# A hybrid decoder layer whose mixer input is scaled by its norm and split a second time, slice by slice

## The chip, the core and the metric

The kernel runs on one core of a Trainium2 chip. The metric is the device time of one execution in microseconds (us), the median of several runs. A core has TensorE (PE, matrix products into PSUM), VectorE (DVE), ScalarE (ACT), GpSimd (POOL) and SyncE (SP, which here only issues transfers). Each engine works through its own list of instructions in a fixed order; semaphores make one wait for another.

## The reference

One decoder layer on 512 tokens of 1024 channels, in float32: `h = x + SwiGLU(norm(x))/2`, then `h = h + mixer(norm(h))`, then `h = h + SwiGLU(norm(h))/2`, then a last norm. The norm before the mixer and the projection behind it are what the change is about:

```
y = xf * lax.rsqrt(jnp.mean(xf * xf, axis=-1, keepdims=True) + EPS); return y * g
proj = (u @ w_in)
(hq, hf, hi, hg, gq, gk, gv, ga, gb, gz, gate_h, gate_g) = jnp.split(proj, offsets)
```

The columns of the projection feed an HGRN2 branch (8 heads; q, forget gate f, values i, output gate g), a gated delta-rule branch (8 key heads, 16 value heads; q, k, v through a short causal convolution, two scalars per head and token, an output gate z) and two merge gates. Each branch is a recurrence over chunks of tokens, gets a norm of its own, is projected back, and the two are merged and projected once more. The root of the norm is one number per token, so it may be applied to the projection's input or to each of its outputs.

## The kernel before

Activations lie channel by token: `h` is eight slices of 128 channels by 512 tokens. A product in float32 is made of three products in a reduced form of float32: both operands are split into a high part (a cast on ScalarE) and a low part (a subtraction on VectorE), and `mm3` (L165 to L168) multiplies high by high, high by low and low by high into one PSUM bank. The split input of the mixer is `uh`, `ul`. Weights come in slabs of 128 by 512 (`raw`, 256 KB), and each slab is cast and subtracted likewise (`whi`, `wlo`, in `maker`, L1865 and L1867).

Before the change `uh` and `ul` hold `h` times the norm's gain, without its root. The root is found while the first columns are being multiplied: sums of squares by token (`pst`, L1971), a power on GpSimd (`rcol`, one number per token in token-major form), a product that spreads it (`pbc`) and a copy (`rbc`, 128 by 512, L1987). Every output of the projection is then multiplied by it when it leaves its bank: by `rbc` on VectorE where the tile is channel by token (`h_q`, `h_f`, `conv`, `tgate`, `decays`), by `rcol` as a factor of ScalarE's activation where it is token by channel (`h_v`, `gate`), and in the two output norms (`h_head`, `g_rec`), where the value columns' factor is still missing.

The order of work is written by a planner, `Desk`, which runs when the program is built: each piece of work is a thread that asks for an engine for a modelled time or for a buffer, and Desk records instructions in the order in which its modelled engines take them. That order is then fixed. The dense columns come in the order of the list `DENSE`, of which `choose` takes the first whose conditions hold: F and Q (forget gate and q of an HGRN head), B (values and gate of two heads), D (the scalars), k, q, v and z of the delta branch, y (the HGRN branch's way back), and where none can be taken, one of 16 merge gate tiles t0 to t15. What it took before the change: F0 Q0 F1 Q1 B0 F2 Q2 F3 Q3 B1 D0 F4 F5 Q4 Q5 B2 F6 F7 t0 Q6 Q7 B3, then k0 to v1, z0, y0 to y7, then the rest of k, q, v and z with t1 to t3 among them, t4 to t15 behind z7, and last the projection of the delta branch (`closing`). Small products of heads and recurrences stand between the large ones.

PSUM has eight banks: two for dense tiles (`mm`), two each in lanes a and b, one each in d and e. A channel-by-token tile is 24 matmuls of 512 columns in one bank; the next tile goes to the other `mm` bank while the first is emptied. B is four such tiles, one per block of 128 tokens, each over all eight slices of the input, so its eight slabs are all needed within its first tile; half of them lie in buffers of their own (`EXTRA`). The first feed-forward block opens differently (`opening`): four tiles in four banks, slice by slice, three matmuls in each bank for each slice.

Of the kernel before, what the change touches and what calls it, by code (L numbers as in the profile page):

```python
# [37 lines left out]
)  # L38
MERGE = (None, None, "a", "a", "b", "b", None, None)
LATE = 1  # L40
WB = 6
EXTRA = ((1, 3, 5, 7), (1, 3, 5, 7), (1, 3, 5, 7), (5, 7))
TA = 6
RB = 3
KEEP = 2
# [76 lines left out]
        assert not self.asked, [(th.rank, th.want) for th in self.asked]  # L122


def body(tc, xT, cst, sqc, hmask, dta, w1o, w1a, w2a, wt, wn, wab, wbh, wbg, wo, w1b, w2b, yT, dbg=None):
    nc = tc.nc
    pe, act, dve, pool, sp = nc.tensor, nc.scalar, nc.vector, nc.gpsimd, nc.sync
    ctx = ExitStack()
# [22 lines left out]
    rcol, rhalf = rcols[:, 0:4], rcols[:, 8:12]  # L151


    def slab(src):
# [662 lines left out]
def mixer(tc, mp, e):  # L817
    nc = tc.nc
    pe, act, dve, pool, sp = nc.tensor, nc.scalar, nc.vector, nc.gpsimd, nc.sync
    cs, ident, tri, strict, hm, ones, mhalf = (e[k] for k in ("cs", "ident", "tri", "strict", "hm", "ones", "mhalf"))  # L820
    uh, ul, rbc, rcols, rcol, rhalf, h = (e[k] for k in ("uh", "ul", "rbc", "rcols", "rcol", "rhalf", "h"))
    psc, dr, dense, slab, wp, mm3, ux, hd, dbg = (
        e[k] for k in ("psc", "dr", "dense", "slab", "wp", "mm3", "ux", "hd", "dbg"))
    wt, wn, wab, wbh, wbg, wo, dta, psd = (e[k] for k in ("wt", "wn", "wab", "wbh", "wbg", "wo", "dtab", "psd"))

    def ps(name, lane="d"):
        return psc.tile([P, T], F32, tag="p" + lane, name=name, bufs=LANES[lane])
# [77 lines left out]
    def decays(pab):  # L905
# [3 lines left out]
        pool.memset(ab, 0.0)  # L909
        z = h[:64, 1]  # L910
        z2 = h[:16, 2]
        yield "on", "rbc"
# [6 lines left out]
        dve.tensor_tensor(z, z, rbc[:64], op=ALU.mult)  # L919
# [62 lines left out]
        D.fire("decays")  # L982


    def h_q(i, pt):
        yield "get", "ta", 2
        yield "on", "rbc"
        yield *V(512), 1
        qs = ta("qs")
        dve.tensor_tensor(qs, pt, rbc, op=ALU.mult)  # L990
# [9 lines left out]
        D.put("ta", 2)  # L1000
        D.fire(("Q", i))

    def h_f(i, pt):
        yield "get", "ta", 1
        yield "on", "rbc"
        yield *V(512), 1
        fs = ta("fs")
        dve.tensor_tensor(fs, pt, rbc, op=ALU.mult)
        D.put("mm")
        yield A(512)  # L1010
        act.activation(fs, fs, AF.Tanh, scale=0.5)
# [12 lines left out]

    def h_v(i, t, o):
        yield A(300)
        act.activation(hv_[i][:, t], o, AF.Copy, scale=rcol[:, t:t + 1])
        if t == 3:
            D.fire(("V", i))

    def h_head(i):
# [148 lines left out]
        yield V(4)  # L1180
        dve.tensor_tensor(rho, rho, rcol, op=ALU.mult)
# [30 lines left out]
    def conv(k, i, pt, out, n):  # L1212

        yield "get", "ta", 2
        yield *V(512), 1
# [3 lines left out]
        D.put("mm")  # L1219
# [234 lines left out]
    def g_rec(u, st):  # L1454
# [95 lines left out]
        yield "use", "POOL", 2.2  # L1550
        pool.tensor_tensor(rho, rho, mhalf[:, :8], op=ALU.pow)
        pool.tensor_tensor(v3(rho, 2), v3(rho, 2), mid(rcol, 2), op=ALU.mult)
        yield "lag", EASE
        ons = []
        for i in range(2):
# [40 lines left out]
    def tgate(i, pt):  # L1596

        yield "get", "ta", 1
        yield *V(512), 1
        g = ta("tg")  # L1600
        dve.tensor_tensor(g, pt, rbc, op=ALU.mult)
        D.put("mm")
        yield A(512)
# [12 lines left out]
        D.put("mm")  # L1616
        D.start((6, d), keep(md[d], g, "ta", ("y", d)))

    def gate(key, g, t, o):

        yield "get", "thg", 1
        yield A(300)
        th = places["thg"]("thg", (P, 256))
        act.activation(th, o, AF.Tanh, scale=rhalf[:, t:t + 1])
        yield V(256)
        dve.scalar_tensor_tensor(g[:, t], th, 1.0, o, op0=ALU.add, op1=ALU.mult)
        D.put("thg")
        if key[0] == "G" or t % 2:
            D.put("mm")
        if t == 3:  # L1630
            D.fire(key)

# [205 lines left out]
    def maker(key, raw):  # L1838
# [31 lines left out]
        yield "lag", .4  # L1870
        D.fire(("slab", key))

    def product():
        for n in range(len(todo) + len(gates) + len(line)):
            yield "on", ("line", n + 1)
            x = k, i = line[n]
            if k == "B":
# [3 lines left out]
                hg_[i] = place("gz", "hg", (P, NT, 256), 4)  # L1881
                for t in range(NT):
                    yield "get", "mm", 1
                    for kt in range(KD):
# [77 lines left out]
    def norm():  # L1962
# [16 lines left out]
        yield V(4)  # L1979
        dve.tensor_scalar(rhalf, rcol, 0.5, None, op0=ALU.mult)  # L1980
        yield "get", "d", 1
        yield T_(.9)
        pb = ps("pbc")
# [72 lines left out]
def layout(i):  # L2056
# [27 lines left out]
    def ffn(n):  # L2084
# [9 lines left out]
        w1a=w1a, w2a=w2a, wt=wt, wn=wn, wab=_kpn(wab).reshape(P, -1),  # L2094
# [18 lines left out]
```

## Time and profile before

| what | value |
|---|---|
| median of 3 runs | 1624.95 us (1624.8 to 1631.92) |
| the profiled execution | 1623.19 us |
| its span, first to last instruction | 1621.4 us |
| TensorE busy | 1599.5 us (99%), 11170 matmul instructions |
| VectorE, ScalarE, GpSimd busy | 1134.0, 858.5, 414.6 us |
| TensorE's granted clock, mean | 0.997 |

An engine's busy time is the sum of its instructions; idle time is put down to what released the engine. PE and PEld are TensorE's matmuls and weight loads. The start of a matmul lies before the end of the one ahead of it, so the distance of starts tells the pace, not the length of one.

### The profile page before, as it was taken

What the parts mean: (1) busy time and instruction counts of PE and PEld (TensorE: products, weight loads), DVE (VectorE), ACT (ScalarE), POOL (GpSimd) and SP (SyncE); (2) the same over time, 40 slices, a digit from 0 to 9 for tenths busy, and PEclk for the clock granted to TensorE, in tenths of its full rate; (3) what the DMA queues carried; (4) which work ended last, traced back from release to release, by engine and by line L of the source; (5) the groups of instructions that cost most, each with busy time, mean ns of one, the idle gap of its engine ahead of it and who ended that gap; (6) DMA issues with size and microseconds to landing.
All of it is one profiled execution on the core that took longest, in us unless ns stands there. A gap on an engine that the chain in (4) does not pass through costs nothing.

```text
span 1621.4 us, 30263 instructions
## 1 busy us (share of the span) xinstructions
PE 1599.5 (99%) x11170; PEld 1408.9 (87%) x11170; DVE 1134.0 (70%) x2166; ACT 858.5 (53%) x1853; POOL 414.6 (26%) x744
## 2 busy tenths in 40 slices
PE   8999999999999999999999999999999999999997
PEld 7999998887878788888888988888888899999887
DVE  7877774547677778658888888755545877778353
ACT  7766663332434435456566565553325766667232
POOL 0222210101121221254571666510001322220012
PEclk9999999999999999999999999999999999999999
DMA  5988843532312222443323333445545888883343
GB/s 177 236 185 183 183 104 98 172 114 86 104 40 73 88 76 90 129 147 98 102 90 110 104 102 121 150 137 185 159 143 163 192 201 183 184 185 79 115 136 117
DMA packets 128165, 216.52 MB, mean 134 GB/s; under 512 B 21888, under 2 KB 27776, under 8 KB 128016
## 3 DMA queue, kind: packets, MB, share of 16 engines
q1 hardware_dynamic: 110448, 182.89, 35.6%
q0 software_dynamic: 17280, 31.46, 12.8%
q8 instruction: 88, 1.44, 0.4%
q14 instruction: 61, 0.50, 0.1%
q10 hardware_dynamic: 288, 0.22, 0.1%
HBM read 197.45 MB, written 17.07 MB: 132 GB/s over the span
## 4 chain that ended last, share of the span: by engine, by line
PE 92%; DMA 3%; issue 1%; ACT 1%; DVE 1%; POOL 0%; SPq 0%; DVEq 0%; ACTq 0%; POOLq 0%
PE pmm L166 16%; PE pmm L167 15%; PE pmm L168 15%; PE pnat L166 4%; PE pnat L168 4%; PE pnat L167 4%; PE pfa L166 3%; PE pfa L167 3%; PE pfa L168 3%; PE pfx L166 2%; PE pfx L168 2%; PE pfx L167 2%; PE pfy L168 2%; PE pfy L167 2%; PE pfy L166 2%
## 5 line engine op out<-in xcount | busy, mean ns | idle before, releaser
L166 PE MATMUL pmm<-uh,whi 128*128 128x512 f32 x632 | 264.4, 418 | 5.6 <-ACT whi L709 5.6
L1865 ACT CAST whi<-raw 128x512 fp32r<-128x512 f32 x226 | 140.1, 620 | 214.5 <-PE pmm L167 156.8
L1867 DVE TENSOR_TENSOR wlo<-raw,whi 128x512 fp32r<-128x512 f32 x226 | 160.6, 711 | 128.3 <-ACT whi L1865 121.8
L168 PE MATMUL pmm<-uh,wlo 128*128 128x512 f32 x632 | 248.2, 393 | 0.0
L167 PE MATMUL pmm<-ul,whi 128*128 128x512 f32 x632 | 247.9, 392 | 0.0
L420 DVE TENSOR_TENSOR sig<-h,sig 128x1024 fp32r<-128x1024 f32 x80 | 97.7, 1221 | 70.4 <-ACT sig L418 70.4
L166 PEld LDWEIGHTS pmm<-uh,whi 128*128 128x128 f32 x632 | 119.5, 189 | 27.1 <-ACT whi L709 5.6
L168 PEld LDWEIGHTS pmm<-uh,wlo 128*128 128x128 f32 x632 | 119.2, 189 | 26.3
L166 PE MATMUL pmm<-gh,whi 128*128 128x512 f32 (+1 forms) x374 | 140.9, 377 | 0.0
L168 PE MATMUL pmm<-gh,wlo 128*128 128x512 f32 (+1 forms) x374 | 140.9, 377 | 0.0
L167 PE MATMUL pmm<-gl,whi 128*128 128x512 f32 (+1 forms) x374 | 140.8, 377 | 0.0
L167 PEld LDWEIGHTS pmm<-ul,whi 128*128 128x128 f32 x632 | 119.7, 189 | 20.4 <-DVE ul L193 0.2
L418 ACT CAST sig<-h 128x1024 fp32r<-128x1024 f32 x80 | 83.9, 1049 | 88.1 <-PE pfa L168 85.1
L204 POOL TENSOR_TENSOR acc<-acc,sqt 128x512 f32<-128x512 f32 x18 | 24.1, 1338 | 376.4 <-ACT sqt L202 376.3
L166 PE MATMUL pnat<-whi,uh 128*128 128x256 f32 (+1 forms) x328 | 107.7, 328 | 0.0
L162 DVE TENSOR_TENSOR wlo<-raw,whi 128x512 fp32r<-128x512 f32 x74 | 54.9, 746 | 67.6 <-ACT whi L161 66.9
L168 PE MATMUL pnat<-whi,ul 128*128 128x256 f32 (+1 forms) x328 | 100.6, 307 | 0.0
L167 PE MATMUL pnat<-wlo,uh 128*128 128x256 f32 (+1 forms) x328 | 100.4, 306 | 0.0
L395 POOL DMA_DIRECT2D wlo<-w1b x63 | 54.5, 868 | 145.9 <-ACT s L470 101.3
L168 PE MATMUL pfa<-th,sig 128*128 128x256 f32 x320 | 90.9, 284 | 0.6 <-DVE sig L420 0.5
L166 PE MATMUL pfa<-th,sig 128*128 128x256 f32 x320 | 91.0, 284 | 0.4 <-ACT s L475 0.4
L167 PE MATMUL pfa<-tl,sig 128*128 128x256 f32 x320 | 90.7, 283 | 0.0
(489 smaller groups left out, 4566.1 us busy)
## 6 DMA issues: line engine op xcount, KB each, us to landing
raw<-wt SPq DMA_DIRECT2D x128, 256.0 KB
raw<-w1b SPq DMA_DIRECT2D x88, 256.0 KB
raw<-w1a SPq DMA_DIRECT2D x80, 256.0 KB
raw<-wn SPq DMA_DIRECT2D x64, 256.0 KB
wlo<-w1b POOLq DMA_DIRECT2D x63, 256.0 KB, 5.9
wlo<-w1a POOLq DMA_DIRECT2D x57, 256.0 KB, 5.5
raw<-w2b SPq DMA_DIRECT2D x45, 256.0 KB
raw<-w2a SPq DMA_DIRECT2D x40, 256.0 KB
```

The costliest lines, as they stand in the source:

```text
L162: dve.tensor_tensor(lo[:, :f], raw[:, :f], hi[:, :f].bitcast(F32), op=ALU.subtract)
L166: pe.matmul(pt, ah, bh, start=first, stop=False, **kw)
L167: pe.matmul(pt, ah, bl, start=False, stop=False, **kw)
L168: pe.matmul(pt, al, bh, start=False, stop=last, **kw)
L204: add.tensor_tensor(acc, acc, s, op=ALU.add)
L395: pool.dma_start(lo, src_, accum_op=ALU.add)
L418: act.copy(hl[:, 0:2], s)
L420: dve.tensor_tensor(hl[:, 2:4], s, hl[:, 0:2].bitcast(F32), op=ALU.subtract)
L1865: act.copy(hi, raw)
L1867: dve.tensor_tensor(lo, raw, hi.bitcast(F32), op=ALU.subtract)
```

## The change

The first two heads' F and Q tiles become one step, S0, made as the feed-forward opening is: the slabs come slice by slice (`wm`, the same weights in another arrangement), and each slice is multiplied into four banks, two of `mm` and both of lane a. When S0 is through with a slice and the root is there, a new thread, `renorm`, writes the slice again: `h` times gain times `rbc` on VectorE, the cast on ScalarE, the subtraction on VectorE. B0 then runs slice by slice too, in both banks of lane b and those of d and e, and waits for each renewed slice. From there on all columns come out of the matmul with the root already in them. Only S0's four tiles are still multiplied by `rbc` (`raw=True`). The other F, Q and gate tiles go through the tanh straight from their bank, the convolution's tiles are copied out by ScalarE, values by a plain copy, gates with a constant factor, and the products by `rcol` in the two output norms are gone. B0 needs no slab buffers of its own.

```
 DENSE = (
-    "F0 Q0 F1 Q1 B0 F2 Q2 F3 Q3 B1 D0 F4 Q4 F5 Q5 B2 F6 Q6 F7 Q7 B3 "
+    "S0 B0 F2 Q2 F3 Q3 B1 D0 F4 Q4 F5 Q5 B2 F6 Q6 F7 Q7 B3 "
...
-EXTRA = ((1, 3, 5, 7), (1, 3, 5, 7), (1, 3, 5, 7), (5, 7))
+EXTRA = ((), (1, 3, 5, 7), (1, 3, 5, 7), (5, 7))
...
     def conv(k, i, pt, out, n):
-        yield *V(512), 1
+        yield *A(512), 1
         ci = ta("ci", (P, T + 32))[:, :T + 3]
+        act.copy(ci[:, 3:], pt)
+        D.put("mm")
+        yield *V(1), 1
         dve.memset(ci[:, :3], 0.0)
-        dve.tensor_tensor(ci[:, 3:], pt, rbc, op=ALU.mult)
-        D.put("mm")
...
     def tgate(i, pt):
-        yield *V(512), 1
+        yield *A(512), 1
         g = ta("tg")
-        dve.tensor_tensor(g, pt, rbc, op=ALU.mult)
+        act.activation(g, pt, AF.Tanh, scale=0.5)
         D.put("mm")
-        yield A(512)
-        act.activation(g, g, AF.Tanh, scale=0.5)
...
+    def renorm(kt):
+        yield "on", "rbc"
+        yield "get", "ta", 1
+        yield V(560)
+        w = ta("un")
+        dve.scalar_tensor_tensor(w, h[:, kt], cs[:, C_MX + kt:C_MX + kt + 1], rbc, op0=ALU.mult, op1=ALU.mult)
+        yield A(512)
+        act.copy(uh[:, kt], w)
+        yield V(512)
+        dve.tensor_tensor(ul[:, kt], w, uh[:, kt].bitcast(F32), op=ALU.subtract)
+        D.put("ta")
+        D.fire(("un", kt))
...
+            if k == "S":
+                yield "get", "mm", 2
+                yield "get", "a", 2
+                ps_ = [psd.tile([P, T], F32, tag="mm", name="pmm") for _ in range(2)] + [ps("pmm", "a") for _ in range(2)]
+                for kt in range(KD):
+                    yield "on", ("slab", (x, kt))
+                    hi, lo = made[x, kt]
+                    for o, pt in enumerate(ps_):
+                        yield T_(.69)
+                        c = slice(o * P, (o + 1) * P)
+                        mm3(pt, hi[:, c], lo[:, c], *ux(kt), kt == 0, kt == KD - 1)
+                    D.put("w")
+                    D.start((0, kt), renorm(kt))
...
+                if i == 0:
+                    lanes = "b", "b", "d", "e"
...
+                    for kt in range(KD):
+                        yield "on", ("slab", (x, kt)), ("un", kt)
+                        for t, pt in enumerate(ps_):
+                            yield T_(.69)
+                            ts = slice(t * P, (t + 1) * P)
+                            mm3(pt, uh[:, kt, ts], ul[:, kt, ts], *made[x, kt], kt == 0, kt == KD - 1)
```

The planner makes a new order from this for all engines of the mixer. What it takes now: S0 B0 F2 F3 B1 Q2 Q3 D0 F4 F5 t0 t1 Q5 Q4 B2 F6 F7 t2 Q6 Q7 B3, k0 to v1, z0, y0 to y7, then the rest of k, q, v and z with t3 and t4 among them, and t5 to t15 behind z7.

TensorE before, where Q1 ends (`pmm`) and B0's first tile (`pnat`) begins; a number behind a name tells one tile or buffer from the next:

```order
L166 MATMUL pmm_4151<-uh_71,whi_4047 128x512
L167 MATMUL pmm_4151<-ul_72,whi_4047 128x512
L168 MATMUL pmm_4151<-uh_71,wlo_4046 128x512
L166 MATMUL pnat_4217<-whi_4070,uh_71 128x512
L167 MATMUL pnat_4217<-wlo_4069,uh_71 128x512
L168 MATMUL pnat_4217<-whi_4070,ul_72 128x512
L166 MATMUL pnat_4217<-wx_4083,uh_71 128x512
```

TensorE in the change, where S0's last slice ends and B0's first begins:

```order
L168 MATMUL pmm_3958<-uh_71,wlo_4048 128x512
L166 MATMUL pmm_3959<-uh_71,whi_4049 128x512
L167 MATMUL pmm_3959<-ul_72,whi_4049 128x512
L168 MATMUL pmm_3959<-uh_71,wlo_4048 128x512
L166 MATMUL pnat_4189<-whi_4073,uh_71 128x512
L167 MATMUL pnat_4189<-wlo_4072,uh_71 128x512
L168 MATMUL pnat_4189<-whi_4073,ul_72 128x512
L166 MATMUL pnat_4190<-whi_4073,uh_71 128x512
```

Before, one bank takes a new slab every three matmuls; now four banks take three matmuls each from one slab.

VectorE before, where the first tiles of F and Q are multiplied by `rbc` among slabs for B0:

```order
L1867 TENSOR_TENSOR wlo_4046<-raw_4012,whi_4047 128x512
L1008 TENSOR_TENSOR fs_4060<-pmm_3977,rbc_74 128x512
L1015 TENSOR_SCALAR f_4072<-fs_4060,cf_3941 128x512
L1867 TENSOR_TENSOR wlo_4069<-raw_4023,whi_4070 128x512
L1020 TENSOR_SCALAR ke_4085<-fs_4060,cf_3941 128x512
```

VectorE in the change, the last two renewed slices (`un`, `ul`), slabs for B0 and the evictions of S0's tiles:

```order
L1881 SCALAR_TENSOR_TENSOR un_4169<-h_70,cs_75,rbc_74 128x512
L1869 TENSOR_TENSOR wlo_4162<-raw_4120,whi_4163 128x512
L1885 TENSOR_TENSOR ul_72<-un_4169,uh_71 128x512
L1869 TENSOR_TENSOR wlo_4193<-raw_4132,whi_4194 128x512
L1881 SCALAR_TENSOR_TENSOR un_4205<-h_70,cs_75,rbc_74 128x512
L1010 TENSOR_TENSOR fs_4185<-pmm_3956,rbc_74 128x512
L1885 TENSOR_TENSOR ul_72<-un_4205,uh_71 128x512
L989 TENSOR_TENSOR qs_4223<-pmm_3957,rbc_74 128x512
```

The evictions of S0 stand behind the renewed slices, and three of the four behind the last of them.

VectorE before, at the last two gate tiles (`tg`) ahead of the last projection, whose slabs are the `wlo`:

```order
L1601 TENSOR_TENSOR tg_13463<-pmm_13384,rbc_74 128x512
L1867 TENSOR_TENSOR wlo_13475<-raw_13378,whi_13476 128x512
L1681 SCALAR_TENSOR_TENSOR mi_13397<-mt_13398,mi_13397 128x512
L1681 SCALAR_TENSOR_TENSOR mi_13399<-mt_13400,mi_13399 128x512
L1867 TENSOR_TENSOR wlo_13496<-raw_13428,whi_13497 128x512
L1601 TENSOR_TENSOR tg_13510<-pmm_13456,rbc_74 128x512
```

ScalarE in the change at the same tiles; the banks are now emptied here, among casts of slabs and of the projection's input (`uh<-og`):

```order
L1603 ACTIVATE tg_13439<-pmm_13370 128x512
L1487 ACTIVATE sqj_13448,sm_11455<-x4_8069 128x128
L1867 CAST whi_13460<-raw_13366 128x512
L1867 CAST whi_13481<-raw_13410 128x512
L1603 ACTIVATE tg_13484<-pmm_13435 128x512
L1649 CAST uh_71<-og_12177 128x512
L1649 CAST uh_71<-og_12839 128x512
L1867 CAST whi_13506<-raw_13442 128x512
```

VectorE's product is gone, and ScalarE's tanh, which stood behind it, reads the bank.

## Rows read from the trace of the kernel before

**Rows 1.** The page: span, and each engine's busy time and instructions.
```profile
span 1621.4 us, 30263 instructions
PE 1599.5 (99%) x11170; PEld 1408.9 (87%) x11170; DVE 1134.0 (70%) x2166; ACT 858.5 (53%) x1853; POOL 414.6 (26%) x744
```

**Rows 2.** Busy time by stretch: the mixer's three parts, and 50 us of gapless matmuls.
```profile
core 0: us, PE busy (x) PEld busy (x) DVE busy (x) ACT busy (x) POOL busy (x), PEclk, DMA share, GB/s
358.00:600.00 242.00, 242.00 (x2116) 195.76 (x2114) 176.52 (x464) 94.58 (x216) 47.27 (x58) 1.00 0.25 76
600.00:1125.00 525.00, 524.56 (x3735) 452.55 (x3734) 401.98 (x930) 301.17 (x836) 229.82 (x533) 1.00 0.38 119
1125.00:1265.00 140.00, 139.09 (x621) 114.97 (x621) 76.58 (x117) 54.19 (x89) 10.00 (x8) 1.00 0.51 162
1150.00:1200.00 50.00, 50.00 (x223) 41.39 (x222) 25.96 (x40) 14.13 (x24) 0.00 (x0) 1.00 0.57 179
```

**Rows 3.** What TensorE waited for between 345 and 1265 us, whole list.
```profile
PE pmm L166 <- DVE tg L1601: 0.9, 1, 0.9
PE ptv L1372 <- DVE gqm L1316: 0.4, 1, 0.4
```

**Rows 4.** Timeline of TensorE: start, length (us), after small matmuls, at two places.
```profile
362.61 0.48 PE L166 MATMUL pmm<-uh,whi 128*128 128x512 f32 x1
362.93 0.40 PE L167 MATMUL pmm<-ul,whi 128*128 128x512 f32 x1
...
1102.76 0.58 PE L166 MATMUL pmm<-uh,whi 128*128 128x512 f32 x1
1103.17 0.40 PE L167 MATMUL pmm<-ul,whi 128*128 128x512 f32 x1
```

**Rows 5.** Timeline of TensorE in the feed-forward opening: two matmuls, twelve apart.
```profile
10.75 0.39 PE L166 MATMUL pmm<-uh,whi 128*128 128x512 f32 x1
...
13.47 0.39 PE L166 MATMUL pmm<-uh,whi 128*128 128x512 f32 x1
```

**Rows 6.** Timeline at the mixer's start: first split of a slice, copy of the root.
```profile
360.49 0.75 DVE L193 SCALAR_TENSOR_TENSOR ul<-h,cs,uh 128x512 fp32r<-128x512 f32 x1 [0.24 <-ACT uh L192]
...
366.58 0.59 ACT L1987 COPY rbc<-pbc 128x512 f32<-128x512 f32 x1 [0.51 <-PE pbc L1985]
```

**Rows 7.** Durations by group: ns min/median/max, or us busy and mean ns.
```profile
L1218 DVE TENSOR_TENSOR ci<-pmm,rbc x32: 672/691/693, 607.0 to 1018.7; 128x512 f32<-128x512 f32 x32
L1601 DVE TENSOR_TENSOR tg<-pmm,rbc x16: 674/684/693, 558.1 to 1128.3; 128x512 f32<-128x512 f32 x16
L1604 ACT ACTIVATE tg<-tg x16: 622/632/633, 558.8 to 1129.1; 128x512 f32<-128x512 f32 x16
L1615 ACT COPY yh<-pmm x8: 577/580/581, 664.3 to 706.3; 128x512 f32<-128x512 f32 x8
L1865 ACT CAST whi<-raw 128x512 fp32r<-128x512 f32 x222 | 137.6, 620 | 208.4 <-PE pmm L167 152.6 <-PE pnat L168 19.2 <-issue 15.1
L1867 DVE TENSOR_TENSOR wlo<-raw,whi 128x512 fp32r<-128x512 f32 x223 | 157.7, 708 | 124.9 <-ACT whi L1865 118.4 <-PE ptv L1372 2.1 <-PE po L1146 1.5
```

**Rows 8.** Timeline where the last recurrence ends and the last projection begins.
```profile
1115.51 0.39 PE L1524 MATMUL pog<-x,x 128*128 128x128 f32 x2
1120.59 0.64 POOL L1552 TENSOR_TENSOR sm<-sm,rcol 128x8 f32<-128x8 f32 x1
1121.08 0.68 DVE L1601 TENSOR_TENSOR tg<-pmm,rbc 128x512 f32<-128x512 f32 x1
1123.15 0.32 SPq L1590 DMA_DIRECT2D td<-tg  x1
1128.33 0.69 DVE L1601 TENSOR_TENSOR tg<-pmm,rbc 128x512 f32<-128x512 f32 x1 [1.72 <-DMA td<-tg]
1129.07 0.50 PE L166 MATMUL pmm<-sogb,whi 128*128 128x512 f32 x1 [0.91 <-DVE tg L1601]
1135.34 0.60 PE L1568 MATMUL pto<-sq,on 128*128 128x128 f32 x4
```

More of the change, by code (lines that the diff above doesn't have):

```diff
@@ L122, in run, with body @@
         assert not self.asked, [(th.rank, th.want) for th in self.asked]
-def body(tc, xT, cst, sqc, hmask, dta, w1o, w1a, w2a, wt, wn, wab, wbh, wbg, wo, w1b, w2b, yT, dbg=None):
+def body(tc, xT, cst, sqc, hmask, dta, w1o, w1a, w2a, wm, wt, wn, wab, wbh, wbg, wo, w1b, w2b, yT, dbg=None):
     nc = tc.nc
@@ L150, in body @@
     rcols = cp.tile([P, 16], F32, name="rcol")
-    rcol, rhalf = rcols[:, 0:4], rcols[:, 8:12]
+    rcol = rcols[:, 0:4]
     def slab(src):
@@ L820, in mixer @@
     cs, ident, tri, strict, hm, ones, mhalf = (e[k] for k in ("cs", "ident", "tri", "strict", "hm", "ones", "mhalf"))
-    uh, ul, rbc, rcols, rcol, rhalf, h = (e[k] for k in ("uh", "ul", "rbc", "rcols", "rcol", "rhalf", "h"))
+    uh, ul, rbc, rcols, rcol, h = (e[k] for k in ("uh", "ul", "rbc", "rcols", "rcol", "h"))
     psc, dr, dense, slab, wp, mm3, ux, hd, dbg = (
         e[k] for k in ("psc", "dr", "dense", "slab", "wp", "mm3", "ux", "hd", "dbg"))
-    wt, wn, wab, wbh, wbg, wo, dta, psd = (e[k] for k in ("wt", "wn", "wab", "wbh", "wbg", "wo", "dtab", "psd"))
+    wm, wt, wn, wab, wbh, wbg, wo, dta, psd = (e[k] for k in ("wm", "wt", "wn", "wab", "wbh", "wbg", "wo", "dtab", "psd"))
     def ps(name, lane="d"):
@@ L982, in decays, with h_q @@
         D.fire("decays")
-    def h_q(i, pt):
-        yield "get", "ta", 2
-        yield "on", "rbc"
-        yield *V(512), 1
-        qs = ta("qs")
-        dve.tensor_tensor(qs, pt, rbc, op=ALU.mult)
-        D.put("mm")
-        yield A(512)
+    def h_q(i, pt, lane="mm", raw=False):
+        yield "get", "ta", 1 + raw
+        qs = pt
+        if raw:
+            yield "on", "rbc"
+            yield *V(512), 1
+            qs = ta("qs")
+            dve.tensor_tensor(qs, pt, rbc, op=ALU.mult)
+            D.put(lane)
+        yield *A(512), 1
         th = ta("th")
@@ L999, in h_q, with h_f @@
         dve.scalar_tensor_tensor(qq[:, :, :P], v3(th, NT), 1.0, v3(qs, NT), op0=ALU.add, op1=ALU.mult)
-        D.put("ta", 2)
+        if not raw:
+            D.put(lane)
+        D.put("ta", 1 + raw)
         D.fire(("Q", i))
-    def h_f(i, pt):
+    def h_f(i, pt, lane="mm", raw=False):
         yield "get", "ta", 1
-        yield "on", "rbc"
-        yield *V(512), 1
         fs = ta("fs")
[L1008 to L1011, printed above, removed]
+        if raw:
+            yield "on", "rbc"
+            yield *V(512), 1
+            dve.tensor_tensor(fs, pt, rbc, op=ALU.mult)
+            D.put(lane)
+        yield *A(512), 1
+        act.activation(fs, fs if raw else pt, AF.Tanh, scale=0.5)
+        if not raw:
+            D.put(lane)
         yield "get", "at", 1
@@ L1026, in h_v @@
         yield A(300)
-        act.activation(hv_[i][:, t], o, AF.Copy, scale=rcol[:, t:t + 1])
+        act.copy(hv_[i][:, t], o)
         if t == 3:
@@ L1549, in g_rec @@
         yield "lag", EASE
-        yield "use", "POOL", 2.2
+        yield "use", "POOL", 1.2
         pool.tensor_tensor(rho, rho, mhalf[:, :8], op=ALU.pow)
-        pool.tensor_tensor(v3(rho, 2), v3(rho, 2), mid(rcol, 2), op=ALU.mult)
         yield "lag", EASE
@@ L1598, in tgate @@
         yield "get", "ta", 1
[L1599 removed]
+        yield *A(512), 1
         g = ta("tg")
[L1601 removed]
+        act.activation(g, pt, AF.Tanh, scale=0.5)
         D.put("mm")
[L1603 to L1604 removed]
         if i in stay:
@@ L1617, in branch, with gate @@
         D.start((6, d), keep(md[d], g, "ta", ("y", d)))
-    def gate(key, g, t, o):
+    def gate(key, g, t, o, lane="mm"):
         yield "get", "thg", 1
@@ L1623, in gate @@
         th = places["thg"]("thg", (P, 256))
-        act.activation(th, o, AF.Tanh, scale=rhalf[:, t:t + 1])
+        act.activation(th, o, AF.Tanh, scale=0.5)
         yield V(256)
@@ L1628, in gate @@
         if key[0] == "G" or t % 2:
-            D.put("mm")
+            D.put(lane)
         if t == 3:
@@ L1785, in weights @@
             return [wab]
+        if k == "S":
+            return list(wm)
         src = wbh[i] if k == "y" else wt[{"Q": 0, "F": 8, "q": 16, "k": 24, "v": 32, "t": 48}[k] + i]
@@ L1871, in maker @@
         D.fire(("slab", key))
+    def renorm(kt):
+        yield "on", "rbc"
+        yield "get", "ta", 1
[8 more added lines that the diff above has]
+        D.fire(("un", kt))
     def product():
@@ L1876, in product @@
             x = k, i = line[n]
+            if k == "S":
+                yield "get", "mm", 2
[10 more added lines that the diff above has]
+                    D.start((0, kt), renorm(kt))
+                for o, (th, lane) in enumerate(((h_f, "mm"), (h_q, "mm"), (h_f, "a"), (h_q, "a"))):
+                    D.start((5, n), th(o // 2, ps_[o], lane, True))
+                continue
             if k == "B":
@@ L1881, in product @@
                 hg_[i] = place("gz", "hg", (P, NT, 256), 4)
+                if i == 0:
+                    lanes = "b", "b", "d", "e"
+                    for t in lanes:
+                        yield "get", t, 1
+                    ps_ = [ps("pnat", t) for t in lanes]
+                    for kt in range(KD):
[4 more added lines that the diff above has]
+                            mm3(pt, uh[:, kt, ts], ul[:, kt, ts], *made[x, kt], kt == 0, kt == KD - 1)
+                        D.put("w")
+                    for t, pt in enumerate(ps_):
+                        D.start((1, n), h_v(i, t, pt[:, :256]))
+                        D.start((1, n), gate(("G", i), hg_[i], t, pt[:, 256:], lanes[t]))
+                    continue
                 for t in range(NT):
@@ L1978, in norm @@
         pool.tensor_tensor(rcol, v, mhalf[:, :4], op=ALU.pow)
-        yield V(4)
-        dve.tensor_scalar(rhalf, rcol, 0.5, None, op0=ALU.mult)
         yield "get", "d", 1
@@ L2093, in layout @@
         w1o=w1a[:2].reshape(4, P, KD, P).transpose(2, 1, 0, 3).reshape(KD, P, 512),
-        w1a=w1a, w2a=w2a, wt=wt, wn=wn, wab=_kpn(wab).reshape(P, -1),
+        w1a=w1a, w2a=w2a, wm=wt[[8, 0, 9, 1]].reshape(4, P, KD, P).transpose(2, 1, 0, 3).reshape(KD, P, 512),
+        wt=wt, wn=wn, wab=_kpn(wab).reshape(P, -1),
         wbh=_cols(f["w_branch_hgrn"][0]), wbg=_cols(f["w_branch_gdn"][0]), wo=_cols(f["w_out"][0]),
```

9 lines of the change are left out of this document (2 added, 7 removed).

## The prediction

> **What bounds the kernel now.** I read the page's busy shares first, then busy time by stretch, then what TensorE waited for, then the timeline around the places that the change touches. TensorE is busy 1599.5 us of a span of 1621.4 us; VectorE has 1134.0 us, ScalarE 858.5 us [rows 1]. A whole-span share is an average, so the mixer (about 358 to 1265 us) has to be read by itself. There TensorE is busy 242.00 of 242 us, 524.56 of 525 us and 139.09 of 140 us [rows 2]: 1.35 us idle in 907 us. The list of its waits for this part has two entries, 0.9 us and 0.4 us [rows 3]. So the mixer is a gapless stream of TensorE instructions, and what VectorE, ScalarE and GpSimd do lies under it. The other 21.9 - 1.35 = 20.5 us of idle TensorE time lie in the two feed-forward blocks, which the diff does not touch.
>
> A busy TensorE is not yet one at its pace, so the spacing of starts counts. In the first feed-forward block's opening, where four banks take three matmuls each in turn, 12 matmuls of 512 columns take 13.47 - 10.75 = 2.72 us [rows 5], 0.2267 us each, at a granted clock of 1.00 [rows 2]. Behind a group of small matmuls the first large one takes longer to hand over: 362.93 - 362.61 = 0.32 us after the sums of squares, 1103.17 - 1102.76 = 0.41 us in the recurrence [rows 4], so 0.09 to 0.18 us more than 0.2267.
>
> **The change part by part.**
>
> TensorE's work. Both programs hold 9786 matmuls of the same shapes: S0 is F0, Q0, F1 and Q1 (96 matmuls), only slice by slice in four banks; B0 keeps its 96. The opening's pace [rows 5] is that of just this pattern, so S0 and B0 take 96 x 0.2267 = 21.8 us each, as before. What differs is how often small groups interrupt the large matmuls: 249 times before, 232 times in the change, counted in the two orders, since nothing but one head fits into B0 and later groups stand together. 17 x 0.09 = 1.5 us to 17 x 0.18 = 3.1 us less; I take 0.14 each, the middle: **-2.4 us**. This is the only term that lies on the bound engine for certain.
>
> The second split. Eight times a product on VectorE, a cast on ScalarE, a subtraction on VectorE: near 0.75 us (the nearest row is the same kind of instruction, product and subtraction by one slice [rows 6]), 0.62 us and 0.71 us [rows 7]. The spread norm is ready at 366.58 + 0.59 = 367.17 us [rows 6]; the first slice is then done near 369.3 us. S0 ends at E, not before 358 + 21.8 = 379.8 us. The last slice can be rewritten only when S0 has read it: made by E + 0.62 + 0.71 = E + 1.3 us, behind one eviction that is queued ahead of it E + 2.0 us. B0 asks for it at E + 7 x 2.72 = E + 19.0 us: 17 us of cover. B0's first slice is needed at E, over 10 us after it is made. Cost 0. If all eight were held until S0's end, TensorE would wait 1.3 us once (0.62 + 0.71), since each following slice costs VectorE about 1.5 us and TensorE 2.72 us. Bounds 0 and 1.3 us; I take 0, as over 10 us of cover would have to vanish. Behind the second product on VectorE stand only slabs of B0 and S0's own evictions; all eight slabs of S0 are split ahead of it, so S0 does not wait for the norm.
>
> The evictions. VectorE loses 32 + 16 + 12 + 1 = 61 products of 512 columns at 0.69 us [rows 7], 42 us, and gains 8 x 0.75 + 8 x 0.71 = 11.7 us. ScalarE gains 32 copies, near 0.58 us (the copy of the y columns out of the same banks [rows 7]), and 8 casts: 23.5 us. The 16 gate tiles and 12 of the F and Q tiles lose a step in a row of two, and their bank is freed by the tanh itself, 0.63 us after its start rather than 0.69 us [rows 7]. Between 600 and 1125 us ScalarE goes from 301 to about 320 of 525 us and VectorE from 402 to about 370 [rows 2]. None of this is on TensorE's path while a bank comes free within the 24 x 0.2267 = 5.44 us of the next tile in the other bank: 0. The spared products of four or eight numbers on VectorE and GpSimd lie in chains that TensorE does not wait for: 0.
>
> The wait that goes. The one wait of 0.91 us is at 1129.07 us [rows 8]: the first columns of the last projection need the bank of gate tile 15, whose product stood on VectorE until the store of tile 14 had landed and given back its buffer (issue 1123.15 us, product at 1128.33 us, so 5.2 us). Now tile 14's tanh comes straight out of the bank, without the product of 1121.08 us ahead of it: its store is issued 0.7 us or more earlier, and the last step is 0.63 us. Of 0.91 us nothing to 0.2 us should stay: **-0.9 us**, at worst 0. What is late next is ScalarE's queue: the tanh of tile 15 now stands ahead of three casts for the last projection, which that projection wants 5.44 us later, so it is covered.
>
> New waits. An order made from modelled times leaves some: 1.35 us in the mixer now. The rearranged order may leave 0, or some of the size seen here; I take one of the largest seen, **+0.9 us**, and keep 0 and 5.4 us (one tile's time, if a bank is once a whole tile late) as ends.
>
> Sum against the profiled execution's own 1623.19 us, of which the span is 1621.4 us and 1.8 us lie around it: 1623.19 - 2.4 - 0.9 + 0.9 = 1620.8 us. The median of the runs shown, 1624.95 us, lies 1.76 us above that execution, so the forecast is 1622.5 us.
>
> **The rivals.**
>
> *Hidden slack in TensorE, faster.* Busy may hide waiting. The weight loads are busy 41.39 of 50 us, 82.8%, where nothing waits, and 195.76 of 242 us, 80.9%, in the stage of the HGRN heads [rows 2]. If the difference is slack and the change removes all of it, that is 242 x (1 - 80.9/82.8) = 5.5 us: 1619.4 us. The Trainium skill, "Perfetto Trace Analysis", § Identifying the Most-Contended Engine, says that matmul busy share is a poor measure and load-weights busy share a good one; by that rule this rival is the headroom there is. Against it: that stage also holds many matmuls under 512 columns with loads of their own, and between 600 and 1125 us the share is 86.2%. Even so it stays within 0.5% (8.1 us).
>
> *Later heads, less filler, slightly slower.* S0 and B0 end four banks at a time and hold them long, among them both banks of lane b, which head 1 needs, until B0 is done. The planner's line shows it: F2 F3 B1 Q2 Q3 in place of F2 Q2 F3 Q3 B1, and three gate tiles spent by B3, not one; 11 of 16 are left behind the last z, not 12: 5.44 us less cover for the last recurrence. If that were needed whole: 1628 us. Against it: the last recurrence's matmul is at 1115.51 us, its norm is done at 1121.2 us, and its transposes are wanted at 1135.34 us [rows 8]; in the change 78 matmuls, 17.7 us, stand between the same two places, not 81. So there are 17.7 - 5.5 = 12 us, less the scaling and queueing of one head, to lose first. The Trainium skill, "Perfetto Trace Analysis", § Matmuls, advises to rotate independent matmul groups through banks so that one's eviction lies beside the next one's matmuls; by that rule S0 and B0, which end four groups together, give something back, and this rival is where it would show.
>
> *ScalarE as gatekeeper, slower than before.* 60 banks in the mixer are now freed by ScalarE in its fixed order, behind casts that wait for weights and exponentials that wait for transfers. Place: 600 to 1120 us, tiles k, q, v and t. Price: one late eviction as the one seen, 0.91 us [rows 3]; from the twelfth on, 10.9 us on top of the forecast, the change is slower by 0.5%; with one tile in four, 15 of 60, 13.7 us: 1636 us. For it: the one wait of this kind comes from just such a queue. Against it: ScalarE is under 62% busy there and the y tiles, evicted by ScalarE already, show no wait in the list [rows 3].
>
> That the change does not do what it says is half true: 32 of the 61 products are not spared but become copies on ScalarE. With TensorE as the bound this changes no time.
>
> **How the numbers follow.** Forecast 0.78 (1618 to 1627 us); hidden slack 0.06; later heads 0.07; ScalarE as gatekeeper 0.06; something faster than any row supports 0.03. A difference under 0.5%, 8.1 us, can't be told from none: below 1616.8 us counts as faster, above 1633.1 us as slower. Faster: 0.03 and a little of hidden slack, 0.04. Slower: 0.06, and 0.01 for later heads with a wait on top, 0.07. The same: 0.89. The range of 8 in 10 goes from 1617 us (all of the hidden slack and the last wait too) to 1631 us (later heads with some new waits).
>
> **What would show it.** Right: TensorE's idle time between 358 and 1265 us stays under 3 us; S0 and B0 run at 2.72 us a slice with no idle before B0's first matmul; VectorE's busy time falls by about 30 us and ScalarE's rises by about 20 us with no effect on the span; the wait before the last projection is gone. Wrong: a wait of several us at the start of B0 (second split late), waits of TensorE for copies of the convolution tiles (gatekeeper), idle time before the last projection's third quarter (later heads), or a spacing other than 0.2267 us in S0 or B0.

## The result and the profile after

The changed kernel took 1628.34 us (median; 1625.62 to 1634.55), the kernel before 1624.88 us beside it: ratio 1.0019, 95% interval 1.0012 to 1.0027. Two later sets of rounds gave 1.0006 (0.9996 to 1.0015) and 1.0008 (0.9999 to 1.0018). The ratios stand 0.05 to 0.2%, 1 to 3 us, above the kernel before, but only the first interval lies clear of 1, and b_wm below, the instructions of before unchanged, came out at 0.9991 (0.9982 to 0.9999): so a ratio can be off by about 0.1%. The change costs between nothing and some 3 us, and none of its three sets shows a gain. The forecast had called a difference this small none, and its sign was wrong: it had 2.4 us less than the profiled execution of before.

The page after (span; busy time, share and instructions of each engine) answers to [rows 1]:
```profile
span 1626.0 us, 30283 instructions
PE 1599.6 (98%) x11170; PEld 1410.4 (87%) x11170; DVE 1108.5 (68%) x2112; ACT 869.2 (53%) x1893; POOL 418.5 (26%) x736
```
TensorE does the same work in the same busy time; VectorE lost 25.5 us and ScalarE gained 10.7 us. The span grew all the same. The stretches of [rows 2], columns as there:
```profile
358.00:600.00 242.00, 240.28 (x2008) 196.11 (x2010) 170.00 (x433) 94.44 (x223) 46.52 (x54) 1.00 0.25 81
600.00:1125.00 525.00, 524.10 (x3852) 452.16 (x3845) 382.17 (x905) 311.98 (x869) 232.51 (x530) 1.00 0.37 115
1125.00:1265.00 140.00, 138.61 (x615) 114.44 (x614) 74.90 (x116) 52.49 (x87) 9.89 (x8) 1.00 0.50 162
```
The idle time of TensorE has a part in each stretch now. What it waited for in the mixer, the whole list, against two entries in [rows 3]:
```profile
PE pnat L166 <- DVE qq L998: 1.6, 1, 1.6
PE pmm L166 <- ACT tg L1603: 1.4, 1, 1.4
PE pq L1423 <- ACT acc L1416: 0.9, 1, 0.9
```
That is 3.9 us for 1.35. From its first matmul (358.08 us before, 359.96 us after) to the end of its last projection the mixer takes 899.94 us before and 901.90 us after. Less the waits it is 898.59 and 897.99 us.

The spans of this pair of executions differ by 4.6 us: 2.0 us in the mixer, 1.9 us ahead of it and 0.8 us behind it. Outside the mixer both programs have the same instructions. Busy time and granted clock (the number behind the count) ahead of the mixer, after:
```profile
45.00:50.00 5.00, 4.00 (x28) 1.00 1.07 308
50.00:55.00 5.00, 4.51 (x24) 0.66 0.90 182
```
before:
```profile
45.00:50.00 5.00, 4.51 (x31) 1.00 1.07 310
50.00:55.00 5.00, 4.42 (x36) 1.00 1.06 212
```
and in b_wm below, which is the kernel before with one tensor more that nothing reads:
```profile
45.00:50.00 5.00, 3.77 (x27) 1.00 1.07 308
50.00:55.00 5.00, 4.13 (x20) 0.68 0.91 198
```
In these rows TensorE stands idle for up to 1.2 of 5 us, and in some executions the clock is at its lower level (1.2 of 2.4 GHz) for part of the next 5 us. b_wm reaches the mixer at 359.66 us, b_tail, with the same feed-forward block, at 357.94 us; b_slack7 and b_slack9, without the change and without the extra tensor, at 359.83 and 359.58 us. So a difference of this size comes without the change, and the traces are compared over the mixer alone.

**Wait one: a Q tile's bank.** Timeline after (start, length, engine, line; in brackets the idle time and what ended it):
```profile
515.50 0.40 PE L168 MATMUL pmm<-uh,wlo 128*128 128x512 f32 x1
...
516.22 0.59 ACT L993 ACTIVATE th<-pmm 128x512 f32<-128x512 f32 x1
516.35 0.69 DVE L1869 TENSOR_TENSOR wlo<-raw,whi 128x512 fp32r<-128x512 f32 x1 [0.88 <-PE po L1150]
...
517.09 0.54 DVE L1024 TENSOR_SCALAR ke<-fs,cf 128x512 f32<-128x512 f32 x1
...
517.55 1.28 DVE L998 SCALAR_TENSOR_TENSOR qq<-th,pmm 128x512 f32<-128x512 f32 x2
...
518.28 0.50 PE L166 MATMUL pnat<-whi,uh 128*128 128x512 f32 x1 [1.62 <-DVE qq L998]
```
The tile is complete near 515.9 us. Its bank used to be free after one product on VectorE; now the tanh on ScalarE and then qq on VectorE, behind a weight's subtraction, gx and ke, must both read it.

**Wait two: the last gate tiles.**
```profile
1123.69 0.59 ACT L1603 ACTIVATE tg<-pmm 128x512 f32<-128x512 f32 x1
1124.12 0.38 SPq L1672 DMA_DIRECT2D mt<-td  x1
1124.60 0.43 SPq L1831 DMA_DIRECT2D raw<-wbg  x1
1125.08 0.61 SPq L1678 DMA_DIRECT2D mg<-td  x1
1126.67 0.32 SPq L1592 DMA_DIRECT2D td<-tg  x1
...
1132.26 0.60 ACT L1603 ACTIVATE tg<-pmm 128x512 f32<-128x512 f32 x1 [3.02 <-DMA td<-tg]
...
1132.91 0.50 PE L166 MATMUL pmm<-sogb,whi 128*128 128x512 f32 x1 [1.39 <-ACT tg L1603]
```
The matmul ahead of this wait starts at 1131.13 us, before at 1127.78 us, so the programs stand 3.35 us apart here. Tile 14's tanh begins at 1123.69 - 3.35 = 1120.34 us in before's time, 0.74 us ahead of the product of [rows 8], just as forecast. The store still goes out at 1126.67 - 3.35 = 1123.32 us, against 1123.15 us: SyncE has the merge's loads (`mi`, `mt`, `mg`) and a weight ahead of it in both programs. Before, around the same tile:
```profile
1120.84 0.58 SPq L1678 DMA_DIRECT2D mg<-td  x1
1121.85 0.63 ACT L1604 ACTIVATE tg<-tg 128x512 f32<-128x512 f32 x1 [1.41 <-DVE tg L1601]
1122.55 0.33 SPq L1829 DMA_DIRECT2D raw<-wbg  x1
```
The tanh ends at 1122.48 us and the store is issued 0.67 us later; in the change it is issued 2.39 us behind its tanh's end.

**Wait three: the inverse behind a weight.**
```profile
943.77 0.69 PE L1413 MATMUL pq<-h,gn 32*32 32x32 f32 x32
...
946.32 0.62 ACT L1867 CAST whi<-raw 128x512 fp32r<-128x512 f32 x1 [2.46 <-DMA raw<-wt]
...
946.84 0.73 ACT L1416 COPY acc<-pq 32x256 f32<-32x256 f32 x2
...
947.63 0.69 PE L1423 MATMUL pq<-acc,gtp 32*32 32x32 f32 x32 [0.90 <-ACT acc L1416]
```
The copies that TensorE needs could start near 944.5 us, but stand in ScalarE's queue behind the cast of a weight that lands near 946.3 us.

### The profile page after: what moved, and what is told of

Read it like the earlier page. It is cut to its first block, busy times and chain, and to the rows that moved or that the text cites. A ratio compares the mean times of both kernels' runs of the same rounds, so it can differ in the third digit from the quotient of the medians.

```text
span 1626.0 us, 30283 instructions
## 1 busy us (share of the span) xinstructions
PE 1599.6 (98%) x11170; PEld 1410.4 (87%) x11170; DVE 1108.5 (68%) x2112; ACT 869.2 (53%) x1893; POOL 418.5 (26%) x736
## 4 chain that ended last, share of the span: by engine, by line
PE 92%; DMA 3%; DVE 2%; issue 1%; ACT 1%; POOL 0%; POOLq 0%; SPq 0%; ACTq 0%; DVEq 0%
PE pmm L166 16%; PE pmm L168 15%; PE pmm L167 15%; PE pnat L166 4%; PE pnat L168 4%; PE pnat L167 4%; PE pfa L166 3%; PE pfa L167 3%; PE pfa L168 3%; PE pfx L166 2%; PE pfx L168 2%; PE pfx L167 2%; PE pfy L168 2%; PE pfy L167 2%; PE pfy L166 2%
## 5 line engine op out<-in xcount | busy, mean ns | idle before, releaser
L1869 DVE TENSOR_TENSOR wlo<-raw,whi 128x512 fp32r<-128x512 f32 x230 | 161.7, 704 | 154.5 <-ACT whi L1867 151.6
L166 PE MATMUL pnat<-whi,uh 128*128 128x256 f32 (+1 forms) x344 | 114.6, 333 | 1.6 <-DVE qq L998 1.6
L168 PE MATMUL pnat<-whi,ul 128*128 128x256 f32 (+1 forms) x344 | 106.8, 311 | 0.0
L167 PE MATMUL pnat<-wlo,uh 128*128 128x256 f32 (+1 forms) x344 | 106.6, 310 | 0.0
```

What stands on the lines that cost most here:

```text
L166: pe.matmul(pt, ah, bh, start=first, stop=False, **kw)
L167: pe.matmul(pt, ah, bl, start=False, stop=False, **kw)
L168: pe.matmul(pt, al, bh, start=False, stop=last, **kw)
L1869: dve.tensor_tensor(lo, raw, hi.bitcast(F32), op=ALU.subtract)
```

## The experiments

In all of them "mixer" is the time from its first matmul to the end of its last projection in the profiled execution; "waits" is what TensorE's list of waits there adds up to, and "low clock" is (1 - granted clock) times busy time, over 5 us windows of the mixer below 0.97.

| kernel | waits us | low clock us | mixer us | mixer less both | ratio (95%) |
|---|---|---|---|---|---|
| before | 1.35 | 0 | 899.94 | 898.59 | 1 |
| b_wm | 1.58 | 0 | 900.28 | 898.70 | 0.9991 (0.9982-0.9999) |
| b_tail | 1.02 | 0 | 899.88 | 898.86 | 1.0000 (0.9991-1.0009) |
| b_slack9 | 1.63 | 0 | 900.76 | 899.13 | 1.0004 (0.9995-1.0014) |
| b_slack7 | 3.04 | 0 | 902.54 | 899.50 | 1.0032 (1.0019-1.0045) |
| b_S | 6.98 | 2.83 | 911.05 | 901.24 | 1.0058 (1.0044-1.0072) |
| the change | 3.91 | 0 | 901.90 | 897.99 | 1.0019 (1.0012-1.0027) |
| a_again | 4.10 | 1.60 | 903.63 | 897.93 | 1.0006 (0.9996-1.0015) |
| a_third | 3.19 | 0 | 901.11 | 897.92 | 1.0008 (0.9999-1.0018) |
| a_both | 2.66 | 0 | 900.87 | 898.21 | 1.0001 (0.9993-1.0010) |
| a_all3 | 1.38 | 0 | 899.49 | 898.11 | 1.0008 (0.9999-1.0017) |
| a_cast | 1.65 | 0 | 900.10 | 898.45 | 1.0006 (0.9997-1.0015) |
| a_slack9 | 6.41 | 2.88 | 909.14 | 899.85 | 1.0052 (1.0037-1.0067) |
| a_convV | 8.46 | 2.78 | 911.08 | 899.84 | 1.0070 (1.0055-1.0085) |

The table is the main finding: without waits and low clock the mixers of all these kernels lie within 3.3 us of each other; waits and low clock make 10 us between them.

**a_again and a_third: the change again.**

> The changed kernel itself once more. Theory W (the time went into three new TensorE waits in the mixer, which the order of instructions fixes): the same three waits stand at the same places, 1.6 us on VectorE's last step of a Q tile near 518 us, 0.9 us near 948 us, 1.4 us near 1133 us, and the ratio to the kernel before is again 1.0012 to 1.0027. Theory L (the extra input tensor moves the others in memory, and the feed-forward blocks pay): the mixer's first matmul is again near 360.0 us, not 358.1 us. If neither holds, the waits or the 1.9 us ahead of the mixer were of one execution only.

> The changed kernel a third time, on the chip of a_cast and beside the same runs of before. Theory W: waits of 3.4 to 5 us at the same three places, mixer less waits and less what a low clock takes 897.8 to 898.1 us (before 898.6 us), ratio 1.0006 to 1.0020. If the waits were not what the time is made of: the same waits with a ratio under 1.0003.

The same three waits in all three executions: 1.6 us at the Q tile each time, 1.4, 0.9 and 1.0 us at the gate tile, 0.9, 1.6 and 0.6 us at the inverse. The order fixes their places; what a transfer takes in that execution sets two of their sizes. The mixer less both agrees within 0.1 us. The ratio that theory W expected of a_again, 1.0012 to 1.0027, did not come back (1.0006); a_third has the ratio expected of it, with waits a little under those expected. Theory L's mark, 360.0 us, came back as 359.2 and 359.1 us. In a_again the wait at the inverse was followed by a low clock (columns as above):
```profile
944.00:948.00 4.00, 2.37 (x39) 1.00 0.18 62
948.00:950.00 2.00, 2.00 (x22) 0.64 0.58 138
950.00:952.00 2.00, 2.00 (x6) 0.51 0.46 132
```
Behind that wait of 1.63 us the low clock took 1.60 us more; in the first execution, after 0.90 us, nothing.

**b_wm: the extra tensor alone.**

```diff
-def body(tc, ..., w2a, wt, ...
+def body(tc, ..., w2a, wm, wt, ...      # wm is never read
```


> The kernel before with the change's extra input tensor declared at its place and never read; no instruction changes. Theory L: ratio 1.0012 or more, the mixer's first matmul near 360.0 us. Theory W: ratio 1.0000 (0.9993 to 1.0007), first matmul near 358.1 us.

The ratio, 0.9991, is not above 1: theory L falls. Its first matmul at 359.66 us goes with the idle time and the clock shown above. The interval, 0.9982 to 0.9999, leaves out 1 although no instruction differs; so one such interval proves no difference of 0.1%.

**a_both: two waits taken away.**

```diff
 h_q: +        if i % 2 and not raw:
      +            qs = mp.tile(...); dve.tensor_copy(qs, pt)
 keep:          sp.dma_start(to, tile_)
      +         D.fire(("st", event))
 merged: -  yield "on", ("K", 7), ...
         +  yield "on", ("K", 7), ..., ("st", ("t", 14))
```


> The changed kernel with the odd Q tiles copied out of their bank by VectorE at once (so the bank is not held until tanh and product are done) and with the store of gate tile 14 issued ahead of the loads for the merge. TensorE's order stays word for word. Theory W: the waits of 1.6 us near 518 us and 1.4 us near 1133 us go, 3.0 us of 1626, so the ratio to the kernel before falls from 1.0019 to 1.0000 (0.9992 to 1.0008). Theory L, or a cost in the spacing of the matmuls: the waits go, but the ratio stays at 1.0010 or more. Rival W2 (the waits only move on): the list of TensorE's waits in the mixer still adds up to over 3 us.

```profile
PE pq L1423 <- ACT acc L1416: 2.0, 1, 2.0
PE pmm L166 <- ACT uh L1649: 0.3, 1, 0.3
PE pmm L167 <- DVE ul L1651: 0.3, 1, 0.3
```
Both waits are gone, so their causes are shown: the bank held through two engines, and the store's place in SyncE's queue. The third grew to 2.0 us here, and operands behind the gate tiles come up with 0.6 us. The mixer is 0.2 to 2.8 us shorter than in the three executions of the change; the ratio, 1.0001, stands beside 1.0006 of the change in the same rounds, and the intervals overlap: the ratios don't show the gain.

**b_tail: the store alone, in the kernel before.** The last two edits of a_both.

> The kernel before with only the store of gate tile 14 ahead of the merge's loads, TensorE's order as before. If that wait (0.91 us in one execution of this order, 1.58 us in another) comes from the store's place in SyncE's queue, it goes and at most 0.6 us on the operands behind it comes up, as in a_both: mixer 898.6 to 899.5 us, ratio 0.9990 to 0.9999. If it comes from the product on VectorE, as the prediction had it, the wait stays at 0.7 us or more and the ratio is 1.0000.

```profile
PE pmm L166 <- ACT uh L1649: 0.4, 1, 0.4
PE ptv L1372 <- DVE gqm L1316: 0.3, 1, 0.3
PE pmm L167 <- DVE ul L1651: 0.3, 1, 0.3
```
The wait of [rows 8] goes with VectorE's product left in place. The store now follows its tanh at once:
```profile
1121.59 0.63 ACT L1604 ACTIVATE tg<-tg 128x512 f32<-128x512 f32 x1 [1.36 <-DVE tg L1601]
1122.25 0.33 SPq L1590 DMA_DIRECT2D td<-tg  x1
```
So the place of the store made the wait, not the product. Most of the gain is taken back by the operands (0.7 us): the mixer takes 899.88 us, 0.4 us more than expected, and the ratio is 1.0000.

**a_all3 and a_cast: the third wait.** A weight's cast and subtraction are held until the next copies to acc are issued; the two runs differ in which weight.

```diff
 maker: +  held = [cast to hi, subtraction to lo]
        +  hold = key == (("z", 1), 2)        # a_cast: (("v", 13), 0)
           yield V(512)
        +  late.extend(held) if hold else ...
 level32, behind the copies to acc:
        +  [late.pop(0)() for _ in late[:]]
```


> The changed kernel with all three of its waits taken away, TensorE's order word for word as in the change: the odd Q tiles copied out at once, the store of gate tile 14 ahead of the merge's loads (both as in a_both), and near 946 us one weight cast and its subtraction issued behind the two copies that the inverse waits for, not ahead of them. Theory W: waits in the mixer under 1.0 us, mixer 898.5 to 899.2 us long (change: 901.9 and 903.6 us, before: 899.9 us), ratio 0.9990 to 1.0000. Rival W2 (a wait moves on): again over 2 us of waits, ratio 1.0000 or more.

> a_both with one more step, at the right place this time: the weight cast of tile v13 and its subtraction (a_all3 held back one of tile z1 instead) are issued behind the two copies to acc that the inverse near 946 us waits for. TensorE's order word for word as in the change. Theory W: the wait of 0.9 to 2.0 us on acc goes, under 1.0 us of waits is left, mixer 898.5 to 899.3 us long (a_both 900.9 us, before 899.9 us), ratio 0.9990 to 1.0000. Rival W2 (the transfer that the cast waits for is late in any case, and TensorE then waits for the slab itself a few matmuls on): the list shows 0.5 to 2 us at wlo or whi near 948 us, ratio 1.0000 or more.

a_all3 held back the wrong weight; the wait came out at 0.8 us by itself. In a_cast the wait on acc is gone: that matmul starts at 944.64 us. Another wait begins 2.7 us later, behind the same weight, in VectorE's queue:
```profile
946.35 0.69 DVE L1867 TENSOR_TENSOR wlo<-raw,whi 128x512 fp32r<-128x512 f32 x1 [3.62 <-ACT whi L1867]
...
947.57 0.68 DVE L1377 TENSOR_TENSOR gvb<-ptv,sm 128x512 f32<-128x512 f32 x1
...
948.30 1.13 PE L1313 MATMUL pgq<-h 128*128 128x256 f32 x4 [1.00 <-DVE gvb L1377]
```
Rival W2 holds in substance: the transfer that lands late is the cause, and the cast only the first to meet it. Both runs miss what theory W expected: 1.4 and 1.65 us of waits are left, not under 1.0, and the ratios, 1.0008 and 1.0006, lie above 1.0000. Neither is faster than the kernel before, nor is any other kernel here whose instructions differ from it.

**b_S: one part alone.** S0 and B0 slice by slice, no second split, the products as before.

```diff
-    "F0 Q0 F1 Q1 B0 F2 Q2 ...
+    "S0 B0 F2 Q2 ...
 (product(), weights(), gate(), h_f(), h_q(): as in the change, without renorm and with the products)
```


> One part alone: the kernel before with S0 and B0 slice by slice in four banks and the change's extra input, but no second split and every eviction with its product as before. Theory W in the form that the later tiles' evictions make the waits (a Q tile's bank held through two engines): none of the change's 1.6 us near 518 us, ratio 0.9985 to 1.0005. Theory O (any new order of this planner leaves new waits, whatever the evictions): waits in the mixer of 2 to 5 us at other places, ratio 1.0008 to 1.0030. Theory L: at least 1.0012 without new waits.

The slowest kernel with the old evictions, 0.58% or some 9 us over the kernel before and slower than either theory had it. The first entries of its list:
```profile
PE pgq L1310 <- DVE ci L1217: 2.6, 1, 2.6
PE pmm L166 <- ACT uh L1575: 1.6, 2, 0.8
```
The 1.6 us on a Q tile is absent, as the evictions' theory has it, yet the new order alone leaves more than the change does, 6.98 us.

**b_slack7, b_slack9, a_slack9: other orders of the same instructions.**

```diff
-SLACK = 0.8
+SLACK = 0.7        # 0.9
```


> The kernel before, evictions and all as they were, with one constant of the planner changed (SLACK 0.7 for 0.8), which only puts the same instructions in another order from the GDN tiles on. Theory O (any new order of this planner leaves new TensorE waits, whatever the evictions): 2 to 7 us of waits in the mixer where before has 1.35 us, ratio 1.0008 to 1.0050. Theory E (the changed evictions make the waits): at most 2 us of waits, ratio 0.9993 to 1.0007.

> The same with SLACK 0.9. Theory O: 2 to 7 us of waits at other places than with 0.7, ratio 1.0008 to 1.0050. Theory E: at most 2 us, ratio 0.9993 to 1.0007.

> The changed kernel with SLACK 0.9: same evictions as the change, another order (the y tiles earlier, Q5 and Q4 apart). Theory O: the waits differ from the change's in place and sum (1 to 7 us, none of them certain to return), ratio 1.0000 to 1.0050. Theory E: the wait on VectorE's last step of a Q tile and one on a tanh or copy by ScalarE return, 3 to 4 us in all, ratio 1.0010 to 1.0027.

b_slack7 has one wait, the gate tile's of [rows 8], grown from 0.91 to 3.0 us by the order; b_slack9 stays below theory O's 2 us and at 1.0004, as theory E has it. a_slack9 has the waits that theory E names (1.3 us on a Q tile, 1.0 us on the gate tile, two at acc with 2.7 us) and one of 1.3 us on a convolution tile that it doesn't; its ratio, 1.0052, lies above both theories. So neither theory takes all: the evictions bring the Q tile's wait along, the order decides the rest, and the order of the kernel before is a good one among its neighbours, not the only one: of five other orders here three (b_S, b_slack7, a_slack9) are slower in intervals well clear of 1, the change is in one of its three, and b_slack9 is not.

**a_convV: the convolution tiles back on VectorE.**

```diff
-        yield *A(512), 1
+        yield *V(512), 1
         ci = ta("ci", ...)
-        act.copy(ci[:, 3:], pt)
+        dve.tensor_copy(ci[:, 3:], pt)
```


> The changed kernel with the 32 convolution tiles copied out of their banks by VectorE instead of ScalarE: VectorE gets 32 x 0.69 us back, ScalarE loses 32 x 0.58 us; same order up to the first GDN tiles. If ScalarE is the gatekeeper (its copies queued behind casts that wait for weights): waits between 600 and 1120 us fall below 0.5 us and the ratio falls to 1.0010 or less. If it is not (theory O): the waits there stay or move, ratio 1.0005 to 1.0040; the 1.6 us near 518 us stay in either case.

The first entries of its list:
```profile
PE ptv L1375 <- DVE gqm L1319: 1.8, 1, 1.8
PE pnat L166 <- DVE qq L998: 1.6, 1, 1.6
PE pmm L166 <- ACT uh L1577: 1.6, 2, 0.8
PE pto L1570 <- DVE on L1562: 1.4, 1, 1.4
PE pgq L1313 <- DVE gqm L1319: 1.3, 1, 1.3
```
The opposite of the gatekeeper: the waits behind ScalarE's acc go, and 4.5 us behind VectorE come. The ratio, 1.0070, lies above both theories. This run also has another order of the delta branch's tiles, so what of the 8 us over the change is VectorE's load and what is order stays open.

## Why the prediction was wrong

**What held.** TensorE is the bound. Summed over its groups of instructions, VectorE lost 30 us (1212.4 to 1182.3) as forecast. S0 ends and B0 begins without a gap, at the pace forecast (timeline after, two matmuls twelve apart in S0, at 374.02 and 376.74 us: 2.72 us); the second split hides wholly. No wait stands before the last recurrence's transposes, so "later heads" did not occur. The share of the weight loads in 358 to 600 us is 196.11 of 242 us, 81.0% after 80.9%: the change won no hidden slack. The Trainium skill, "Perfetto Trace Analysis", § Identifying the Most-Contended Engine, judges TensorE's headroom by that share, beside the rate of useful products; headroom of this kind no run here shows.

**The term of -2.4 us for 17 fewer interruptions** was mis-sized. The mixer less waits and low clock is 0.6 to 0.7 us shorter (898.59 against 897.92 to 897.99 us), not 2.4. From start to start, waits left out, the large matmuls (those of `mm3`) take 739.1 us of the mixer before and 736.3 us after, when 226 groups of small matmuls stand among them instead of 242: 2.8 us less, about what I had worked out. But the small matmuls, the same in number, take 161.7 us instead of 159.5 and give 2.2 us of it back. I had counted one side of the hand-over only; why the small ones take longer in their new places is not shown. (In the whole traces the groups are 249 and 233, against 249 and 232 in the prediction; both pages count 11170 matmuls, not 9786.)

**"The wait that goes", -0.9 us,** is a step that failed. The tanh was early by 0.74 us as said, but I had taken the store to follow it. It follows SyncE's queue. By [rows 8] the store went out 1.39 us behind the end of the product (1123.15 - 1121.76 us), 0.76 us more than a tanh of 0.63 us [rows 7] fills, and I did not ask what stood between. The wait became 0.9 to 1.4 us; b_tail shows the queue as its cause.

**"Their bank is freed by the tanh itself"** is wrong for the six Q tiles, whose bank is read once more by qq; a wait of 1.6 us came from it, on one of the six, in every execution of the change, and went in a_both. The diff shows it: the put of the bank moved behind qq, and there without the priority that the product had. Here a bank that two engines read one after the other was held through both their queues.

**"New waits", +0.9 us**, with 0 and 5.4 us as ends, was mis-sized: 3.2 to 4.1 us stand in the list in all, 2.2 to 3.2 us of them at the two new places, and behind one of them the low clock took 1.6 us more. I had priced a wait at its length. The right number lay within the ends; the value taken was the best case seen in an order that had been picked.

**The sum, by what was measured**, in the three executions: -0.6 us of spacing, +1.8 to +2.75 us of waits, 0 or 1.6 us of low clock: +1.2 to +3.7 us, against +1.0 to +3.1 us from the three ratios. So the mixers of the profiled executions are accounted for; the ratios alone would not show it. Taking waits away brought the mixer from 901.1 to 903.6 us down to 899.5 to 900.9 us (a_both, a_all3, a_cast), within 1 us of before. Their ratios are 1.0001 to 1.0008, 1.0005 in the mean, against 1.0011 in the mean of the change's three: that points the same way and is no more than the noise. Whether the change would gain with all its waits away stays open.

## What to carry to other kernels

Where one engine is busy without a gap, as here, an edit elsewhere is worth what it does to that engine's few waits, and the new order that it causes can weigh more than the work it saves: list for every freed bank all readers and the queue in front of each. Read a transfer's issue time from its queue, not only from when its data are ready. Before a planned order's small gain is credited to an edit, run some neighbouring orders of the old program.

## What the runs showed of the hardware

ScalarE's gate tanh was faster with a constant as scale than with a column in memory. Groups of instructions, before (instructions, us busy, mean ns):
```profile
L1624 ACT ACTIVATE thg<-pnat,rcol 128x256 f32<-128x256 f32 x48 | 22.6, 470 | 12.2 <-PE pnat L168 7.4 <-DVE ggz L1626 3.8 <-DVE x L1626 0.7
L1027 ACT ACTIVATE v<-pnat,rcol 128x256 f32<-128x256 f32 x16 | 7.6, 474 | 57.3 <-PE pnat L168 57.2
```
after:
```profile
L1624 ACT ACTIVATE thg<-pnat 128x256 f32<-128x256 f32 x48 | 18.4, 385 | 14.5 <-PE pnat L168 7.8 <-DVE ggz L1626 4.9 <-DVE x L1626 1.5
L1031 ACT COPY v<-pnat 128x256 f32<-128x256 f32 x16 | 5.7, 374 | 28.0 <-PE pnat L168 27.9
```
85 and 100 ns less each, 6.1 us in all; in the second row the operation changed too, from ACTIVATE to COPY. Summed over its groups, as VectorE's time above, ScalarE's grew by 17 us (940.9 to 957.8) and not by the 23.5 us of the prediction, and these 6.1 us are nearly all of the difference. The Trainium skill, "ScalarE: Activation LUTs", § What ACT_TABLE_LOAD costs, gives about 93 ns for each such operand; the trace agrees, and the prediction had overlooked it.

A stop of TensorE of 1.63 us (a_again, 948 to 952 us) was followed by some 3 us of a clock near the lower level; stops of 1.62 us (the change, 518 us) and 2.03 us (a_both, 947 us) were followed by a granted clock of 1.00. So what a wait cost beyond its length differed among these executions.
